# FFN gate and up products of a two-layer decoder: one 512-column pass of the high weights over both token parts, 128 inner columns at a time

## The chip, the cores and the metric

The kernel runs on one core of one Trainium2 chip. The metric is the device time of one execution in microseconds, median of several runs. Engines are named as in the profile: PE (TensorE matmul), PEld (TensorE weight load), DVE (VectorE), ACT (ScalarE), POOL (GpSimd), SP (the queue from which most DMAs are issued).

## What is computed

Two layers of a decoder trunk for 256 tokens of width 1024. Each layer has two feed-forward parts (FFN) with a token mixer between them; only the FFNs change here:

```python
def swiglu(x, w_gate, w_up, w_down):
    return (jax.nn.silu(x @ w_gate) * (x @ w_up)) @ w_down
# x: 256 x 1024; w_gate, w_up: 1024 x 2816; w_down: 2816 x 1024
f1 = swiglu(rms_norm(h, ffn1_pre_g[l]), ffn1_w_gate[l], ffn1_w_up[l], ffn1_w_down[l])
h = h + 0.5 * rms_norm(f1, ffn1_post_g[l])
```

Everything is float32, and the output must keep nearly its precision.

## The kernel before

**Split numbers.** A float32 product is made of three passes of TensorE. Each operand is split in a high part (rounded to the engine's reduced float32 format, `F32R`) and a low part (the rest), and high x high, high x low and low x high are summed in PSUM. `mm3` (L248) does that for products whose moving operand are weights; `gu_cols` (L372) does it where the weights are the stationary operand.

**Weights.** A unit is 1 MB of weights. SP fetches it into one of 3 raw buffers (`fetch`, L201); `prepare` (L215) splits it on ACT (copy to the high part, L227) and DVE (subtraction for the low part, L228), in pieces, into one of 5 ring slots. When TensorE has used a unit for the last time, `done` frees its slot and `pump` prepares and fetches the next, in the order of `specs`.

**Order.** TensorE's order is written by hand as strings (`FFN_FIRST`, `FFN_START`, `FFN_BODY`, `FFN_END`, and a loop at L413 to L417): each name is one step, run in that order. The orders of DVE and ACT are chosen by a scheduler at build time, the work on units at a lower priority; on the chip each engine runs its list strictly in order.

**The FFN.** The 2816 inner columns are 11 blocks of 256, numbered c = 0 to A (hexadecimal).

- c = 0 and 1 (`gu_rows`, steps g and u): the tokens are stationary (`xT`), the weights move; one step is one block of 256 columns for one of the two groups of 128 tokens. The outputs (`pg`, `pu`, one bank of 512 columns per token group) are evacuated by `evac_rows` and transposed by `tr`.
- c = 2 to A (`gu_cols`, steps G and U): the weights are stationary, 128 columns at a time (b = 0, 1), and all 256 tokens move. One step is 2 x 8 x 3 = 48 passes of 256 columns into one bank (`qg`, `qu`); `evac_cols` (step E) then works on 512 columns (both b) at a time and `split` leaves the two parts of `hT`.
- D steps (`down`): 12 passes of 512 columns for one block and one token group, into four banks `facc` that stay for the whole FFN. PSUM has 8 banks, so 4 are left for the rest.

Between FFNs stand the mixers, whose code the change does not touch.

At the start, `x0`, the first unit, `x1` (the second 128 tokens) and the second unit are fetched in this order (L953 to L960); the first unit by one DMA per 128 rows.

Of the kernel before, what the change touches and what calls it, by code (L numbers as in the profile page):

```python
# [14 lines left out]
AF = mybir.ActivationFunctionType  # L15
ALU = mybir.AluOpType
# [3 lines left out]
P = 128  # L20
D = 1024
KD = D // P
S = 256
# [18 lines left out]
"""  # L42
FFN_FIRST = "g00 xb1 g10 g01 g11 sc0 sc1 u00 u01 u10 u11 e0 e1"
FFN_START = "g00 g10 sc0 xb1 u00 u10 e0 g01 g11 sc1 u01 u11 e1"
FFN_BODY = "G2 t0 rsb U2 t1 E2 side D00 D01 D10 D11 G3 U3 E3 D20 D21"
FFN_END = "D80 D90 DA0 fa0 D81 D91 fb0 xb0 DA1 fa1 fb1"
NC = FF // 256

# [38 lines left out]
def trunk(ctx: ExitStack, tc: tile.TileContext, T, out):  # L87
# [54 lines left out]
    def ffn_specs(l, f):  # L142
        wg, wu, wd = (T[f"ffn{f}_w_{n}"][l] for n in ("gate", "up", "down"))

        def gu(nm, c):
            cols_unit((l, f, nm, c), wg if nm == "g" else wu, 0, KD, c * 256, 256)

        def dn(c):
            cols_unit((l, f, "d", c), wd, 2 * c, 2, 0, D)

        for nm in "gu":
            for c in range(2):
                gu(nm, c)
        for c in range(2, NC):
            gu("g", c)
            gu("u", c)
            if c == 2:
                dn(0)
                dn(1)
            elif c < NC - 1:  # L160
                dn(c - 1)
        dn(NC - 2)
        dn(NC - 1)
# [163 lines left out]
    def ffn(l, f, rs, finish, side=None):  # L327
        hr, ev = {}, {}

        def scales(t):  # L330
            hr[t], ev[t] = small("hr", 1), small("ev", 1)
            pool.tensor_scalar(hr[t], rs[t][0], 0.5, None, op0=ALU.mult)
            pool.tensor_scalar(ev[t], rs[t][1], 4.0 * EPS, None, op0=ALU.mult)

        acc = [None, None]
        ps, hT, hs, tmp = {}, {}, {}, {}


        def gu_rows(nm, c, t):
            if c == 0:  # L340
                ps[nm, t] = bank("p" + nm)
            u = units[l, f, nm, c]
            mm3(ps[nm, t][:, c * 256:(c + 1) * 256],
                [(xT[:, 0, t, k, :], xT[:, 1, t, k, :], u[:, 0, k, :], u[:, 1, k, :]) for k in range(KD)],
                True, True)
            if t == 1:
                done((l, f, nm, c))

        def evac_rows(t):
            g, u = ps.pop(("g", t)), ps.pop(("u", t))  # L350
            th = w(t, "th")
            act.activation(th, g, AF.Tanh, scale=hr[t])
            m = w(2 + t, "m")
            dve.scalar_tensor_tensor(m, th, 1.0, g, op0=ALU.add, op1=ALU.mult)
            h = w(4 + t, "h")
            dve.scalar_tensor_tensor(h, u, hr[t], m, op0=ALU.mult, op1=ALU.mult)
            hs[t] = h

        def split(src):
            q = half("hT").rearrange("p (h n) -> p h n", h=2)  # L360
            act.activation(q[:, 0], src, AF.Copy)
            dve.tensor_sub(q[:, 1], src, q[:, 0].bitcast(F32))
            return q

        def tr(t):
            b = bank("ht")
            for k in range(4):
                pe.transpose(b[:, k * P:(k + 1) * P], hs[t][:, k * P:(k + 1) * P], ident)
            hT[t] = split(b)


        def gu_cols(nm, c):  # L372
            o = bank("q" + nm)
            u = units[l, f, nm, c]
            for b in range(2):
                bs = slice(b * P, (b + 1) * P)
                o3 = o[:, b * 256:(b + 1) * 256].rearrange("p (t n) -> p t n", t=NT)
                n = 0
                for k in range(KD):
                    for a, h in ((0, 0), (0, 1), (1, 0)):  # L380
                        pe.matmul(o3, u[:, a, k, bs], xT[:, h, :, k, :], start=n == 0, stop=n == 3 * KD - 1)  # L381
                        n += 1
            ps[nm] = o
            done((l, f, nm, c))

        def evac_cols(c):
            i = c % 2
            b2 = lambda a: a.rearrange("p (b n) -> p b n", b=2)
            g, u = ps.pop("g"), ps.pop("u")
            gp = w(i, "gp")  # L390
            dve.tensor_tensor(b2(gp), b2(g), tmp["rsB"][:, None, :].to_broadcast([P, 2, S]), op=ALU.mult)  # L391
            m = w(2 + i, "m")
            act.activation(m, gp, AF.Tanh, scale=0.5)
            dve.scalar_tensor_tensor(m, m, 1.0, gp, op0=ALU.add, op1=ALU.mult)
            h = w(4 + i, "h")
            dve.scalar_tensor_tensor(h, u, 0.5, m, op0=ALU.mult, op1=ALU.mult)  # L396
            hT["c", c] = split(h)

        def down(c, t):
            if acc[t] is None:  # L400
                acc[t] = acc_tile("facc")
            u = units[l, f, "d", c]
            if c < 2:
                q = [[hT[t][:, a, (2 * c + k) * P:(2 * c + k + 1) * P] for k in range(2)] for a in range(2)]
            else:
                q = [[hT["c", c][:, a, k * 256 + t * P:k * 256 + (t + 1) * P] for k in range(2)] for a in range(2)]
            for j, js in enumerate(HALF):
                mm3(acc[t][j], [(q[0][k], q[1][k], u[:, 0, k, js], u[:, 1, k, js]) for k in range(2)],
                    c == 0, c == NC - 1)
            if t == 1:  # L410
                done((l, f, "d", c))

        order = (FFN_FIRST if side else FFN_START).split() + FFN_BODY.split()  # L413
        for c in range(4, NC):
            order += [f"{n}{c:X}" for n in "GUE"]
            if c < NC - 2:
                order += [f"D{c - 1:X}0", f"D{c - 1:X}1"]  # L417
        order += FFN_END.split()
        for n in order:
            if n == "rsb":  # L420
                tmp["rsB"] = broadcast_rows(rs)
            elif n == "side":
                if side:
                    side()
            elif n[:2] == "fa":
                finish[0](int(n[2]), acc[int(n[2])], ev[int(n[2])])
            elif n[:2] == "fb":
                finish[1](int(n[2]))
            elif n[:2] == "sc":
                scales(int(n[2]))  # L430
            elif n[:2] == "xb":
                if n[2] == "1" or not finish[2]:
                    pre_b(int(n[2]))
            elif n[0] in "gu":
                gu_rows(n[0], int(n[1]), int(n[2]))
            elif n[0] == "e":
                evac_rows(int(n[1]))
            elif n[0] == "t":
                tr(int(n[1]))
            elif n[0] in "GU":  # L440
                gu_cols(n[0].lower(), int(n[1], 16))
            elif n[0] == "E":
                evac_cols(int(n[1], 16))
            else:
                down(int(n[1], 16), int(n[2]))

# [572 lines left out]
```

## Time and profile before

| | |
|---|---|
| median of 3 runs | 994.09 us (992.03 to 998.48) |
| the profiled execution | 992.19 us, of which the profile's span 990.3 us |
| PE busy | 971.3 us (98%), 6678 matmuls |
| DVE busy | 646.6 us (65%) |
| ACT busy | 478.5 us (48%) |
| DMA | 176.04 MB, mean 178 GB/s |
| granted TensorE clock | 0.998 of full |

A matmul's duration in the profile overlaps with the next one's, so what a matmul costs is read from the distance between starts (the pitch), not from its duration. "Busy" of PE counts such overlapped time once.

### The profile page before, as it was taken

Reading aid. Unit: us, or ns where it says so; the run is one execution under the profiler, and the core shown is the slowest. Engines: PE = TensorE matmul, PEld = TensorE weight load, DVE = VectorE, ACT = ScalarE, POOL = GpSimd, SP = SyncE. Lnnn points to the kernel's source line nnn. Section 1 sums busy time; section 2 is a strip of 40 time slices with the busy share of each in tenths; the row PEclk is TensorE's granted clock in tenths of the full one; section 3 lists DMA queues with packets and bytes.
Section 4 is the critical chain, followed back from the end, with each engine's and each line's share of the span. In section 5 each row is a group of like instructions: output and inputs, shape, how many; then the busy total and the mean of one; then the engine's idle time right before and its main releaser. Section 6 shows DMA issues by size and latency. Waiting matters only on the chain.

```text
span 990.3 us, 16105 instructions
## 1 busy us (share of the span) xinstructions
PE 971.3 (98%) x6678; PEld 888.8 (90%) x6678; DVE 646.6 (65%) x864; ACT 478.5 (48%) x760; POOL 80.3 (8%) x136
## 2 busy tenths in 40 slices
PE   6999999999999999999999999999999999999997
PEld 6999999988779999999999999998887799999996
DVE  5785555578988655555677455567799776565552
ACT  5564343457556543443455343345468454443431
POOL 2000000030034000000030000002101320000000
PEclk9999999999999999999999999999999999999999
DMA  7975555456525555555557555553763166655511
GB/s 257 331 227 207 172 201 181 151 163 178 173 72 212 191 190 175 186 195 172 169 174 251 180 189 185 173 204 107 204 189 107 46 211 234 197 186 176 190 61 43
DMA packets 131553, 176.04 MB, mean 178 GB/s; under 512 B 13156, under 2 KB 111768, under 8 KB 131480
## 3 DMA queue, kind: packets, MB, share of 16 engines
q1 hardware_dynamic: 131192, 174.43, 53.6%
q8 instruction: 52, 0.85, 0.3%
q10 hardware_dynamic: 288, 0.59, 0.2%
q14 instruction: 21, 0.17, 0.0%
HBM read 173.95 MB, written 1.05 MB: 177 GB/s over the span
## 4 chain that ended last, share of the span: by engine, by line
PE 94%; DVE 2%; ACT 2%; DMA 1%; issue 0%; SPq 0%; DVEq 0%; POOLq 0%; POOL 0%; ACTq 0%
PE qu L381 21%; PE qg L381 21%; PE facc L251 8%; PE facc L252 8%; PE facc L253 8%; PE pu L251 2%; PE pu L253 2%; PE pu L252 2%; PE pg L252 2%; PE oacc L251 2%; PE pg L253 1%; PE oacc L253 1%; PE oacc L252 1%; PE pg L251 1%; PE yT L766 1%; PE chp L794 1%
## 5 line engine op out<-in xcount | busy, mean ns | idle before, releaser
L227 ACT ACTIVATE unit<-raw 128x1024 fp32r<-128x1024 f32 (+2 forms) x320 | 322.4, 1032 | 357.3 <-issue 301.1
L228 DVE TENSOR_TENSOR unit<-raw,unit 128x1024 fp32r<-128x1024 f32 (+2 forms) x320 | 375.9, 1195 | 138.6 <-ACT unit L227 138.2
L381 PEld LDWEIGHTS qg<-xT,unit 128*128 128x128 f32 x1728 | 211.6, 192 | 2.2
L381 PE MATMUL qu<-xT,unit 128*128 128x256 f32 x1728 | 213.5, 283 | 0.0
L381 PE MATMUL qg<-xT,unit 128*128 128x256 f32 x1728 | 213.0, 283 | 0.0
L381 PEld LDWEIGHTS qu<-xT,unit 128*128 128x128 f32 x1728 | 209.9, 192 | 0.0
L251 PE MATMUL facc<-unit,hT 128*128 128x512 f32 x352 | 137.9, 392 | 0.0
L252 PE MATMUL facc<-unit,hT 128*128 128x512 f32 x352 | 137.3, 390 | 0.0
L253 PE MATMUL facc<-unit,hT 128*128 128x512 f32 x352 | 137.0, 389 | 0.0
L253 PEld LDWEIGHTS facc<-unit,hT 128*128 128x128 f32 x352 | 66.1, 188 | 14.1
L251 PEld LDWEIGHTS facc<-unit,hT 128*128 128x128 f32 x352 | 66.2, 188 | 12.7
L252 PEld LDWEIGHTS facc<-unit,hT 128*128 128x128 f32 x352 | 66.2, 188 | 12.5
L391 DVE TENSOR_TENSOR gp<-qg,rsB 128x512 f32<-128x512 f32 x36 | 24.9, 690 | 67.5 <-PE qg L381 67.5
L396 DVE SCALAR_TENSOR_TENSOR h<-qu,m 128x512 f32<-128x512 f32 x36 | 24.9, 691 | 55.0 <-PE qu L381 55.0
L267 POOL TENSOR_TENSOR mspost<-ev,s 128x1 f32<-128x1 f32 x8 | 4.7, 589 | 677.1 <-ACT sq L261 677.1
L252 PE MATMUL pg<-unit,xT 128*128 128x256 f32 x128 | 37.4, 292 | 1.3 <-DVE unit L228 1.2
L251 PE MATMUL pg<-unit,xT 128*128 128x256 f32 x128 | 37.4, 292 | 0.3 <-ACT unit L227 0.3
L253 PE MATMUL pg<-unit,xT 128*128 128x256 f32 x128 | 37.0, 289 | 0.0
L251 PE MATMUL pu<-unit,xT 128*128 128x256 f32 x128 | 36.5, 285 | 0.0
L253 PE MATMUL pu<-unit,xT 128*128 128x256 f32 x128 | 36.2, 283 | 0.0
L252 PE MATMUL pu<-unit,xT 128*128 128x256 f32 x128 | 36.2, 283 | 0.0
L742 ACT ACTIVATE pr<-s,mx 128x128 f32<-128x128 f32 (+1 forms) x64 | 26.1, 433 | 3.0 <-DVE mx L740 2.9
(259 smaller groups left out, 1162.6 us busy)
## 6 DMA issues: line engine op xcount, KB each, us to landing
raw<-in_ffn_w_down_dram SPq DMA_DIRECT2D x44, 1024.0 KB, 5.1
raw<-in_ffn_w_gate_dram SPq DMA_DIRECT2D x42, 1024.0 KB, 5.0
raw<-in_ffn_w_up_dram SPq DMA_DIRECT2D x42, 1024.0 KB, 5.1
raw<-in_w_in_dram SPq DMA_DIRECT2D x14, 1024.0 KB, 5.1
raw<-in_w_out_dram SPq DMA_DIRECT2D x4, 1024.0 KB, 4.9
raw<-in_w_out_dram SPq DMA_DIRECT2D x8, 512.0 KB, 6.3
raw<-in_w_in_dram SPq DMA_DIRECT2D x4, 560.0 KB, 3.7
raw<-in_ffn_w_up_dram SPq DMA_DIRECT2D x4, 512.0 KB
```

What stands on the lines that cost most here:

```text
L227: act.activation(u[:, 0, i:i + step], r[:, i:i + step], AF.Copy)
L228: dve.tensor_sub(u[:, 1, i:i + step], r[:, i:i + step], u[:, 0, i:i + step].bitcast(F32))
L251: pe.matmul(o, sh, mh, start=first and i == 0, stop=False)
L252: pe.matmul(o, sh, ml, start=False, stop=False)
L253: pe.matmul(o, sl, mh, start=False, stop=last and i == n - 1)
L267: pool.tensor_add(m, eps, s2[:, 0:1])
L381: pe.matmul(o3, u[:, a, k, bs], xT[:, h, :, k, :], start=n == 0, stop=n == 3 * KD - 1)
L391: dve.tensor_tensor(b2(gp), b2(g), tmp["rsB"][:, None, :].to_broadcast([P, 2, S]), op=ALU.mult)
L396: dve.scalar_tensor_tensor(h, u, 0.5, m, op0=ALU.mult, op1=ALU.mult)
L742: act.activation(prs[v][:, b0 + i, :], sb[v][:, i, :], AF.Exp, bias=mx[:, i:i + 1], accum_out=cf[:, v, b0 + i:b0 + i + 1])
L766: pe.matmul(YT[t][v * 64:(v + 1) * 64, :], vsw[kb][:, br, v * 64:(v + 1) * 64], PT.pop((t, br, v, kb)), start=False, stop=br == 1 and kb == t,
L794: pe.matmul(b3, u[:, a, k, cs_], xT[:, h, :, k, :], start=n == 0, stop=n == 3 * KD - 1)
```

## The change

For c = 2 to A, each b now is a step of its own (G20, U20, E20, G21, ...). For each of the 8 row blocks k, the low weights meet the high tokens in a pass of 256 columns, and the high weights meet the high and the low tokens in one pass of 512 columns; the two products lie side by side in one bank and are added when it is evacuated: ACT copies the second half out, DVE adds the first. `evac_cols` works on 256 columns at a time. A unit of gate or up weights is used by two steps and freed after the second.

For c = 0 and 1, the two units of gate (and of up) are the upper and the lower half of the rows, 512 columns wide, in place of two blocks of 256 columns over all rows; `gu_rows` makes passes of 512 columns.

```diff
-FFN_BODY = "G2 t0 rsb U2 t1 E2 side D00 D01 D10 D11 G3 U3 E3 D20 D21"
+FFN_BODY = "G20 t0 rsb U20 E20 G21 t1 U21 E21 side D00 D01 D10 D11 G30 U30 E30 G31 U31 E31 D20 D21"
@@ ffn_specs
-            for c in range(2):
-                gu(nm, c)
+            for h in range(2):
+                cols_unit((l, f, nm, h), wg if nm == "g" else wu, 4 * h, 4, 0, 512)
@@ gu_rows
-            u = units[l, f, nm, c]
-            mm3(ps[nm, t][:, c * 256:(c + 1) * 256],
-                [(xT[:, 0, t, k, :], xT[:, 1, t, k, :], u[:, 0, k, :], u[:, 1, k, :]) for k in range(KD)],
-                True, True)
+            u = units[l, f, nm, h]
+            mm3(ps[nm, t], [(xT[:, 0, t, 4 * h + k, :], xT[:, 1, t, 4 * h + k, :], u[:, 0, k, :], u[:, 1, k, :])
+                            for k in range(4)], h == 0, h == 1)
@@ gu_cols
-            for b in range(2):
-                bs = slice(b * P, (b + 1) * P)
-                o3 = o[:, b * 256:(b + 1) * 256].rearrange("p (t n) -> p t n", t=NT)
-                n = 0
-                for k in range(KD):
-                    for a, h in ((0, 0), (0, 1), (1, 0)):
-                        pe.matmul(o3, u[:, a, k, bs], xT[:, h, :, k, :], start=n == 0, stop=n == 3 * KD - 1)
-                        n += 1
+            bs = slice(b * P, (b + 1) * P)
+            for k in range(KD):
+                pe.matmul(o[:, :S].rearrange("p (t n) -> p t n", t=NT), u[:, 1, k, bs], xT[:, 0, :, k, :],
+                          start=k == 0, stop=False, skip_group_check=True)
+                pe.matmul(o.rearrange("p (h t n) -> p h t n", h=2, t=NT), u[:, 0, k, bs], xT[:, :, :, k, :],
+                          start=False, stop=k == KD - 1, skip_group_check=True)
@@ evac_cols
-            dve.tensor_tensor(b2(gp), b2(g), tmp["rsB"][:, None, :].to_broadcast([P, 2, S]), op=ALU.mult)
-            m = w(2 + i, "m")
+            act.activation(gp, g[:, S:], AF.Copy)
+            act.activation(h, u[:, S:], AF.Copy)
+            dve.tensor_add(gp, g[:, :S], gp)
+            dve.tensor_mul(gp, gp, tmp["rsB"])
             act.activation(m, gp, AF.Tanh, scale=0.5)
+            dve.tensor_add(h, u[:, :S], h)
             dve.scalar_tensor_tensor(m, m, 1.0, gp, op0=ALU.add, op1=ALU.mult)
-            dve.scalar_tensor_tensor(h, u, 0.5, m, op0=ALU.mult, op1=ALU.mult)
-            hT["c", c] = split(h)
+            dve.scalar_tensor_tensor(h, h, 0.5, m, op0=ALU.mult, op1=ALU.mult)
+            split(h, hT["c", c][:, :, bs])
@@ the loop over c = 4 to A
-            order += [f"{n}{c:X}" for n in "GUE"]
+            order += [f"{n}{c:X}{b}" for b in range(2) for n in "GUE"]
```

On PE, at a block in the middle of an FFN, one row of before stands for 48 equal passes (`unit_860` is the block's gate unit, `unit_901` its up unit, `unit_957` a down unit):

```order
L252 MATMUL facc_704<-unit_804,hT_874 128x512
L253 MATMUL facc_704<-unit_804,hT_874 128x512
L381 MATMUL qg_1061<-xT_80,unit_860 128x256 x48
L381 MATMUL qu_1117<-xT_80,unit_901 128x256 x48
L251 MATMUL facc_689<-unit_957,hT_1027 128x512
```

After the change, the same place where step G of b = 0 ends and U of b = 0 begins (`unit_601` is the gate unit, `unit_632` the up unit):

```order
L378 MATMUL qg_776<-xT_80,unit_601 128x256
L380 MATMUL qg_776<-xT_80,unit_601 128x512
L378 MATMUL qu_793<-xT_80,unit_632 128x256
L380 MATMUL qu_793<-xT_80,unit_632 128x512
L378 MATMUL qu_793<-xT_80,unit_632 128x256
```

Each step now alternates 8 passes of 256 and 8 of 512 columns, and a block has four steps (G, U, G, U) in place of two.

On ACT, one block of before (the pieces of three units, L227, stand around the two steps of the evacuation):

```order
L227 ACTIVATE unit_1569<-raw_1421 128x1024
L227 ACTIVATE unit_1625<-raw_1477 128x1024
L361 ACTIVATE hT_1639<-h_1637 128x512
L227 ACTIVATE unit_1625<-raw_1477 128x1024
L227 ACTIVATE unit_1666<-raw_1518 128x1024 x2
```

and a block of the change, from the end of b = 0 to the end of b = 1:

```order
L361 ACTIVATE hT_950<-h_949 128x256
L393 ACTIVATE gp_947<-qg_961 128x256
L227 ACTIVATE unit_978<-raw_846 128x1024 x2
L397 ACTIVATE m_948<-gp_947 128x256
L394 ACTIVATE h_949<-qu_985 128x256
L227 ACTIVATE unit_1002<-raw_870 128x1024 x2
L361 ACTIVATE hT_950<-h_949 128x256
L227 ACTIVATE unit_1043<-raw_911 128x1024 x2
```

The copies out of the banks (L393, L394) are new, and the last part of b = 1 (L361) stands behind both pieces of a unit. From the first `facc` evacuation of an FFN to the first step of the next FFN, the lists of DVE and ACT are the same as before.

On SP, at the start of the program, before:

```order
L953 DMA x0_81<-in_x_dram 128x1024
L210 DMA raw_99<-in_ffn1_w_gate_dram 128x256 x5
L210 DMA raw_99<-in_ffn1_w_gate_dram 128x256 [waits DMAHW0_49]
L210 DMA raw_99<-in_ffn1_w_gate_dram 128x256 [waits DMAHW1_49]
L210 DMA raw_99<-in_ffn1_w_gate_dram 128x256 [waits DMAHW2_49]
L957 DMA x1_82<-in_x_dram 128x1024 [waits DMAHW3_49]
L210 DMA raw_109<-in_ffn1_w_gate_dram 128x4x256 [waits DMAHW4_49]
```

and after (a name behind "waits" is one of eight counters, freed by the landing of an earlier DMA):

```order
L957 DMA x0_81<-in_x_dram 128x1024
L210 DMA raw_99<-in_ffn1_w_gate_dram 128x512 x4
L961 DMA x1_82<-in_x_dram 128x1024
L210 DMA raw_105<-in_ffn1_w_gate_dram 128x2x512 [waits DMAHW0_49]
L210 DMA raw_105<-in_ffn1_w_gate_dram 128x2x512 [waits DMAHW1_49]
```

The first unit is now four DMAs, and `x1` is issued without a wait.

## Rows read from the trace of the kernel before

**Rows 1.** The page's part 1: busy time, share of the span, instructions, by engine.

```profile
PE 971.3 (98%) x6678; PEld 888.8 (90%) x6678; DVE 646.6 (65%) x864; ACT 478.5 (48%) x760; POOL 80.3 (8%) x136
```

**Rows 2.** The page's part 4: the chain that ended last, by engine.

```profile
PE 94%; DVE 2%; ACT 2%; DMA 1%; issue 0%; SPq 0%; DVEq 0%; POOLq 0%; POOL 0%; ACTq 0%
```

**Rows 3.** Waits of PE, whole span: line, releaser, us in total, times, longest us.

```profile
PE xt L311 <- DMA cn<-in_consts_dram: 6.8, 1, 6.8
PE yT L720 <- ACT pcT L715: 2.4, 2, 1.2
PE pg L252 <- DVE unit L228: 1.2, 2, 1.0
```

**Rows 4.** Chain in order of time, one block c: start us, length us, what.

```profile
78.34 5.75 PE qg L381 x48
84.09 5.76 PE qu L381 x48
95.32 5.75 PE qg L381 x48
```

**Rows 5.** Timeline of PE: first and twelfth of a row of 512-column passes.

```profile
300.05 0.39 PE L251 MATMUL oacc<-unit,yA 128*128 128x512 f32 x1
...
302.55 0.39 PE L253 MATMUL oacc<-unit,yL 128*128 128x512 f32 x1
```

**Rows 6.** Windows, one block c: stretch, length, busy by engine, clock, DMA share, GB/s.

```profile
78.30:95.30 17.00, 17.00 (x123) 16.04 (x122) 9.67 (x10) 7.07 (x8) 0.00 (x0) 1.00 0.54 187
```

**Rows 7.** Timeline of PE: first and 34th of a row of gu_rows passes.

```profile
19.03 0.28 PE L253 MATMUL pg<-unit,xT 128*128 128x256 f32 x1
...
22.99 0.28 PE L253 MATMUL pg<-unit,xT 128*128 128x256 f32 x1
```

**Rows 8.** Groups by line and shape: count, busy us, mean ns, idle before, releaser.

```profile
L228 DVE TENSOR_TENSOR unit<-raw,unit 128x1024 fp32r<-128x1024 f32 x304 | 365.0, 1221 | 133.2 <-ACT unit L227 132.9
L391 DVE TENSOR_TENSOR gp<-qg,rsB 128x512 f32<-128x512 f32 x36 | 24.9, 690 | 67.5 <-PE qg L381 67.5
L394 DVE SCALAR_TENSOR_TENSOR m<-m,gp 128x512 f32<-128x512 f32 x36 | 24.7, 685 | 4.2 <-ACT m L393 4.2
L842 DVE SCALAR_TENSOR_TENSOR xc<-xr,prm,xc 128x256 f32<-128x256 f32 x12 | 5.7, 477 | 0.1
L570 DVE TENSOR_TENSOR qr<-qA,qB 128x256 f32<-128x256 f32 x4 | 1.7, 419 | 0.0
L798 DVE TENSOR_TENSOR gl<-chg,rsB 128x256 f32<-128x256 f32 x4 | 1.7, 414 | 0.3 <-PE chg L794 0.3
L393 ACT ACTIVATE m<-gp 128x512 f32<-128x512 f32 x36 | 22.2, 618 | 10.8 <-DVE gp L391 10.7
L361 ACT ACTIVATE hT<-h 128x512 fp32r<-128x512 f32 x36 | 22.1, 614 | 5.1 <-DVE h L396 5.1
L323 ACT ACTIVATE rsB<-rsB 128x256 f32<-128x256 f32 x6 | 2.3, 380 | 0.0
L856 ACT ACTIVATE thi<-gate,hb 128x256 f32<-128x256 f32 x4 | 1.9, 475 | 1.1 <-DVE e L854 1.1
```

**Rows 9.** Timeline, end of the first FFN: first pass of D80, last part of hT.

```profile
186.11 0.40 PE L251 MATMUL facc<-unit,hT 128*128 128x512 f32 x1
...
188.59 0.69 DVE L362 TENSOR_TENSOR hT<-h,hT 128x512 fp32r<-128x512 f32 x1
```

**Rows 10.** Timeline of ACT: a unit's piece right behind the end of step G.

```profile
118.14 1.06 ACT L227 ACTIVATE unit<-raw 128x1024 fp32r<-128x1024 f32 x1 [3.75 <-issue]
```

**Rows 11.** Chain in order of time, the start of the program.

```profile
7.30 5.81 DMA x<-in_x_dram
13.32 0.48 issue
13.80 0.69 DVE xg L278
14.49 0.61 DVE unit L228
15.15 0.38 PE pg L252
```

**Rows 12.** Timeline of SP, and of PE at the first up pass.

```profile
1.16 6.09 SPq L210 DMA_DIRECT2D raw<-in_ffn_w_gate_dram  x8
7.30 0.44 SPq L957 DMA_DIRECT2D x<-in_x_dram  x1
...
25.63 0.28 PE L251 MATMUL pu<-unit,xT 128*128 128x256 f32 x1
```

**Rows 13.** Windows, the start: stretch, length, busy by engine, clock, DMA share, GB/s.

```profile
11.00:13.00 2.00, 2.00 (x11) 2.00 (x11) 0.69 (x2) 0.73 (x3) 1.04 (x4) 1.00 1.07 365
```

More of the change, by code (lines that the diff above doesn't have):

```diff
@@ L336, in ffn, with gu_rows @@
         ps, hT, hs, tmp = {}, {}, {}, {}
-        def gu_rows(nm, c, t):
-            if c == 0:
+        def gu_rows(nm, h, t):
+            if h == 0:
                 ps[nm, t] = bank("p" + nm)
-            u = units[l, f, nm, c]
-            mm3(ps[nm, t][:, c * 256:(c + 1) * 256],
-                [(xT[:, 0, t, k, :], xT[:, 1, t, k, :], u[:, 0, k, :], u[:, 1, k, :]) for k in range(KD)],
-                True, True)
+            u = units[l, f, nm, h]
+            mm3(ps[nm, t], [(xT[:, 0, t, 4 * h + k, :], xT[:, 1, t, 4 * h + k, :], u[:, 0, k, :], u[:, 1, k, :])
+                            for k in range(4)], h == 0, h == 1)
             if t == 1:
-                done((l, f, nm, c))
+                done((l, f, nm, h))
         def evac_rows(t):
@@ L357, in evac_rows, with split @@
             hs[t] = h
-        def split(src):
-            q = half("hT").rearrange("p (h n) -> p h n", h=2)
+        def split(src, q=None):
+            if q is None:
+                q = half("hT").rearrange("p (h n) -> p h n", h=2)
             act.activation(q[:, 0], src, AF.Copy)
@@ L369, in tr, with gu_cols @@
             hT[t] = split(b)
-        def gu_cols(nm, c):
-            o = bank("q" + nm)
+        def gu_cols(nm, c, b):
+            o = ps[nm] = bank("q" + nm)
             u = units[l, f, nm, c]
-            for b in range(2):
-                bs = slice(b * P, (b + 1) * P)
-                o3 = o[:, b * 256:(b + 1) * 256].rearrange("p (t n) -> p t n", t=NT)
-                n = 0
-                for k in range(KD):
-                    for a, h in ((0, 0), (0, 1), (1, 0)):
-                        pe.matmul(o3, u[:, a, k, bs], xT[:, h, :, k, :], start=n == 0, stop=n == 3 * KD - 1)
-                        n += 1
-            ps[nm] = o
-            done((l, f, nm, c))
@@ L389, in evac_cols @@
+            if b == 1:
+                done((l, f, nm, c))
+        def evac_cols(c, b):
+            if b == 0:
+                i = c % 2
+                tmp["w"] = w(i, "gp"), w(2 + i, "m"), w(4 + i, "h")
+                hT["c", c] = half("hT").rearrange("p (h n) -> p h n", h=2)
+            bs = slice(b * S, (b + 1) * S)
+            gp, m, h = (a[:, bs] for a in tmp["w"])
             g, u = ps.pop("g"), ps.pop("u")
-            gp = w(i, "gp")
-            dve.tensor_tensor(b2(gp), b2(g), tmp["rsB"][:, None, :].to_broadcast([P, 2, S]), op=ALU.mult)
@@ L440, in ffn @@
             elif n[0] in "GU":
-                gu_cols(n[0].lower(), int(n[1], 16))
+                gu_cols(n[0].lower(), int(n[1], 16), int(n[2]))
             elif n[0] == "E":
-                evac_cols(int(n[1], 16))
+                evac_cols(int(n[1], 16), int(n[2]))
             else:
```

4 lines of the change are left out of this document (removed).

## The prediction

> **What bounds the kernel now.** I first read the busy shares: PE is busy for 98% of the span, DVE for 65%, ACT for 48% [rows 1]. The chain of work that ended last is PE for 94% [rows 2], and PE's waits sum to little: 6.8 us for the first data, and some 6 us more in the whole span, none inside an FFN after the start [rows 3]. So time falls only where PE's own stream gets shorter, as long as the others keep up. The next question is what a pass costs. Its duration in the profile overlaps with the next one's, so I take the pitch. One step G of 48 passes of 256 columns lasts 5.75 us [rows 4], which is 119.9 ns a pass. Twelve passes of 512 columns start between 300.05 and 302.55 [rows 5]: 2.50 / 11 = 227.3 ns. The D steps of a block agree: from 84.09 + 5.76 = 89.85 to 95.32 are 5.47 us for 24 passes [rows 4], 227.9 ns with the turn to the next step.
>
> At 2.4 GHz (the granted clock of this block is 1.00 [rows 6]) 256 columns stream in 106.7 ns and 512 in 213.3. So a pass costs its columns plus 13 to 14 ns, whether it is short or long. Two passes of 256 cost 239.8 ns, one of 512 costs 227.3: each such pair that becomes one pass saves 12.5 ns. The number of columns that stream does not change; only the number of passes does.
>
> **The term of the change, on PE.**
> - c = 2 to A: 4 FFNs x 9 blocks x 2 (gate, up) x 2 (b) x 8 (k) = 1152 times, three passes of 256 become one of 256 and one of 512: 1152 x 12.5 ns = 14.4 us. A block loses 0.40 us of its 16.98 [rows 4].
> - c = 0 and 1: 4 FFNs x 2 x 2 token groups x 2 units x 24 = 768 passes of 256 become 384 of 512: 384 x 12.5 ns = 4.8 us. Their pitch now is the same as in the blocks: 33 steps between 19.03 and 22.99 are 120.0 ns each [rows 7].
> - Sum 19.2 us. With 227.9 ns for a 512 pass it is 1536 x 11.9 = 18.3; inside a D step alone the pitch would allow 19.5.
>
> What is not in the trace is a 512 pass whose moving rows are four separate pieces of 128 (high and low part, two token groups). Today's block passes read two pieces (119.9 ns), those of `gu_rows` one (120.0), with no difference between them; so I price four pieces at nothing extra. The other unseen thing is the alternation of short and long passes. The turns from G/U to D and back (two per block) are inside the 5.47 us and cost at most 24 x 0.6 ns = 14 ns together, so I take nothing there either.
>
> The Trainium skill speaks against this change. "TensorE: Matmul & The Clock Gate", section "Wait — 56ns, not 53.3ns?", gives the warm pitch as N / 2.4 GHz plus about 2.5 ns. By it 256 columns cost 109.2 ns and 512 cost 215.8, a pair saves 2.5 ns and the whole change 3.8 us, too little to be seen. The trace does not agree: 119.9 and 227.3 ns. I follow the rows; a pass with hardly a cost of its own is the first rival.
>
> **What is added on DVE and ACT, and what hides it.** Per block DVE had four operations of 512 columns at about 688 ns [rows 8], 2.75 us. Now it has six of 256 per b; by the nearest rows 3 x 0.414 (sums and the scaling, L798, L570), 2 x 0.477 (L842) and 0.419 for the low part: 2.62 us, 5.24 per block, 2.5 more, 90 us over 36 blocks. ACT had 0.618 + 0.614; now per b two copies at 0.380 (L323), a tanh at 0.475 (L856) and a copy at 0.380: 3.23 per block, 2.0 more, 72 us in all. A block today has 9.67 us of DVE and 7.07 of ACT in 17.0 [rows 6]; it becomes 12.2 and 9.1 in 16.6. The tightest place is c = 9 and A, which have no D steps between: 11.1 us with two units (9.67 - 2.75 = 6.92 us for three, 2.31 each) and 5.24 of evacuation, 9.9 us, 89%. So both stay under PE and I price them at nothing; beyond that, each microsecond by which a block is late would be one on the path.
>
> Waits: four PSUM banks rotate among G, U, G, U, so a step needs the bank of the step four before it, which ended 8.3 us earlier or more. The evacuation of a bank stands behind at most one unit (two pieces: 1.06 each on ACT [rows 10], 1.22 on DVE [rows 8]), so it takes 3 to 5 us. At the end of an FFN the last hT part is needed by the fourth pass of DA0, 5.46 + 0.68 us after the last U. Today it is ready at 188.59 + 0.69, 3.2 us behind 186.11 [rows 9]; then it stands behind both pieces of a unit on ACT, and by the same rows I get 4.5 to 4.7 us. No wait, 1.5 us to spare.
>
> Ring slots: the gate unit is freed after G of b = 1, 8.3 us into the block instead of 5.76, the up unit at 11.1 as before. Today ACT starts the next unit right when G ends (118.14 [rows 10]), so its data had landed. The slot freed by gate takes the down unit that is needed 16 us after its new preparation; nothing there comes onto the path.
>
> **The start.** x1 is issued at 7.30, behind eight pieces of the first unit of which the later ones wait for counters, and lands 5.81 us later [rows 11, 12]. DVE's work on x1 (`xg`) then stands before the last piece of the first unit, which PE awaits at 15.15. After: five issues at about 0.44 us [rows 12] put x1 at about 3 us. Ahead of it are the gains, x0 and the first unit, 2.1 MB with a little, and itself 0.5 MB; at the 365 GB/s of this stretch [rows 13] that is some 7 us, so I expect it at about 10. On the other side DVE now has two pieces, not one, behind `xg`. Worked through (xg from 11.0, third piece at 12.9, g00 done at 15.1), the first up pass comes at about 24.2 instead of 25.63 [rows 12]; 0.45 of this is already in the 4.8. I take 1 us. If x1 comes no sooner, PE waits for the third piece until 15.1 and the start loses 1 us; if nothing waits, it gains 2.5.
>
> **Sum.** 990.3 - 19.2 - 1.0 = 970.1 us of span; with the 1.9 us around it 972.0. The profiled execution lies 1.9 us under the median of the runs shown, so a median should lie between 972 and 974: I say 973.
>
> **Rivals.**
> 1. *The saving per pass is not there.* The excess is not a pass's own but follows something that stays (the split products summed, the rows read), and the new pair takes what the three passes took, 359.7 ns. For it: no row shows the same stream both ways. Against: 256 and 512 columns show the same excess, 13.2 and 14.0 ns, so an excess that grows with columns is excluded. Time: only the start is left, 992.2 - 1 = 991, by the median 993: no change that can be seen. The Trainium skill's 2.5 ns a pass ("TensorE: Matmul & The Clock Gate") would make it 987 to 989, no change either.
> 2. *The long pass hides more.* If the excess came from loading weights behind a short pass, a pass of 512 would have none, and a triple would cost its 768 columns, 320 ns instead of 359.7: 1152 x 39.7 = 46 us, time 940 to 947. Against: today's 512 passes still carry 14 ns.
> 3. *Evacuation comes late.* ACT and DVE run in order; a unit whose data is late holds the copy out of a bank behind it. With 0.53 us of wait per block the 19 us are gone; half of that gives 982. For it: 89% of DVE at c = 9 and A. Against: the 8.3 us above.
> 4. *Slower: four pieces cost.* If reading high and low tokens from far-apart rows cost a restart per piece, the 512 pass in qg and qu would be dearer. From 227.3 + 16.7 = 244 ns on, the gain is gone (1152 x 16.7 ns = 19.2 us); at 252 it is slower by 1%, about 1002. Against: one piece and two cost the same [rows 4, 7].
>
> **How the numbers follow.** A measurement of this kernel tells about 1% from no change (10 us). Chances: the forecast 0.80 (968 to 978: 18.3 to 19.5 for the passes, -1 to +2.5 for the start, 972 to 974 for the median, and some scatter), rival 1 0.07, rival 2 0.03, rival 3 0.06, rival 4 0.04. Faster by over 1% is the forecast, rival 2 and most of rival 3: 0.87; same is rival 1 and the rest of 3: 0.09; slower 0.04. The range 965 to 982 holds the forecast, with room for its scatter, and the milder half of rival 3.
>
> **What the changed profile would show.** Right: a block c lasts about 16.6 us instead of 16.98, a step G of 16 passes about 2.78 us, matmuls 6678 - 1536 = 5142, DVE near 735 us, ACT near 550, no new waits of PE inside the FFNs, up passes starting at about 24. Wrong would be: blocks at 16.9 (rival 1), at 15.7 (rival 2), PE waiting for `qg` or `qu` banks or for `hT` (rival 3), or 512 passes in qg at over 240 ns (rival 4).

## The result, and the profile after

The changed kernel takes 983.03 us (median, 982.67 to 983.91) against 993.94 us of the kernel before (992.03 to 998.48) on the same chip: a ratio of 0.989, 95% interval 0.987 to 0.9911. It is faster by 10.9 us; the prediction said 973 us, 21 us faster, and 965 to 982 as the range. About half of the expected gain is there. One of the ten runs of an experiment below (the long pass as two short ones) took 1753.75 us at a mean granted clock of 0.78; no ratio here counts it.

The profiled execution took 983.91 us, of which the span is 982.0 us (before 990.3). The page of the kernel after, part 1, and PE's waits (line, releaser, us in total, times, longest us):

```profile
PE 963.9 (98%) x5142; PEld 807.9 (82%) x5142; DVE 716.5 (73%) x1152; ACT 543.0 (55%) x976; POOL 81.2 (8%) x136
```

```profile
PE xt L311 <- DMA cn<-in_consts_dram: 7.5, 1, 7.5
PE yT L724 <- ACT pcT L719: 2.1, 2, 1.2
PE cmpT L678 <- DVE kcb L670: 1.0, 2, 0.6
PE pT L759 <- DVE pr L751: 0.8, 2, 0.4
PE pg L251 <- ACT unit L227: 0.4, 1, 0.4
```

There are 5142 matmuls, as counted in advance, and PE is still busy for 98% of the span [rows 1]. Every wait has its like before, and none lies inside an FFN after the start [rows 3]. So the missing gain is inside PE's own stream. The timeline of PE in a step G of the kernel after (start us, duration us, what) shows it:

```profile
110.14 0.28 PE L378 MATMUL qg<-xT,unit 128*128 128x256 f32 x1
110.26 0.40 PE L380 MATMUL qg<-xT,unit 128*128 128x512 f32 x1
110.49 0.28 PE L378 MATMUL qg<-xT,unit 128*128 128x256 f32 x1
110.61 0.40 PE L380 MATMUL qg<-xT,unit 128*128 128x512 f32 x1
110.85 0.28 PE L378 MATMUL qg<-xT,unit 128*128 128x256 f32 x1
...
111.20 0.28 PE L378 MATMUL qg<-xT,unit 128*128 128x256 f32 x1
...
112.97 0.28 PE L378 MATMUL qu<-xT,unit 128*128 128x256 f32 x1
```

Read the distances between starts. A pair of a short and a long pass takes 0.35, 0.36, 0.35 us and so on; eight pairs from 110.14 to 112.97 are 2.83 us, 353.8 ns a pair. The prediction had 119.9 + 227.3 = 347.2, and the three passes of before took 359.7. So a pair saves 6 ns, not 12.5. The whole block shows the same (window of one block's length, with length, busy time of PE, PEld, DVE, ACT and POOL, granted clock, DMA share, GB/s):

```profile
110.77:127.56 16.79, 16.79 (x90) 14.30 (x89) 11.64 (x18) 8.90 (x15) 0.00 (x0) 1.00 0.57 188
```

It lasts 16.79 us, where 16.98 stood before [rows 4] and 16.58 was expected. DVE has 11.64 us of work in it and ACT 8.90: both have room.

**Where the time went.** The second FFN from its first pass on `pg` to its last on `facc`, after and then before:

```profile
308.43 0.39 PE L251 MATMUL pg<-unit,xT 128*128 128x512 f32 x1
...
494.67 0.39 PE L253 MATMUL facc<-unit,hT 128*128 128x512 f32 x1
```

```profile
309.79 0.28 PE L251 MATMUL pg<-unit,xT 128*128 128x256 f32 x1
...
499.11 0.39 PE L253 MATMUL facc<-unit,hT 128*128 128x512 f32 x1
```

186.24 us and 189.32: 3.08 us less, where 4.8 were expected. With the same two marks the trace splits the whole span (us):

| | before | after | difference | expected |
|---|---|---|---|---|
| to the first `pg` pass | 9.13 | 9.82 | +0.69 | } -5.8 |
| FFN 1 | 193.99 | 190.31 | -3.68 | } |
| FFN 2, 3, 4 | 567.09 | 557.83 | -9.26 | -14.4 |
| mixer 1 | 106.67 | 108.29 | +1.62 | 0 |
| mixer 2 | 106.46 | 109.03 | +2.57 | 0 |
| the rest | | | -0.2 | 0 |
| span | 990.3 | 982.0 | -8.3 | -20.2 |

Three things are short: each FFN by 1.7 us (6.9 together), the start by about 1 us, and both mixers, whose code did not change, are longer by 4.2 us together. In the mixers the granted clock fell; the experiment on the clock, below, shows that this lengthened them. The window of the kernel after around the place where it lost most (same columns), and the chain of waits there:

```profile
745.00:756.00 11.00, 11.00 (x51) 6.04 (x51) 7.74 (x17) 5.51 (x17) 0.00 (x0) 0.69 0.28 95
```

```profile
732.48 1.06 PE s L740 x8
...
744.73 1.12 PE yT L724 x2
...
750.88 2.01 PE s L740 x8
```

The eight passes of L740 take 1.06 us at 732 and 2.01 us at 751, with a mean granted clock of 0.69 between 745 and 756: part of it at 2.4, part at 1.2 GHz. Just ahead PE had waited 1.18 us for ACT (L724). The same place in the profiled run of before has the same wait ahead of `yT` (timeline, first line), but the eight passes behind it (chain, second) last 1.06 us, and the granted clock (window, third) is 1.00:

```profile
752.28 1.12 PE L720 MATMUL yT<-pcT,vb 32*128 32x512 f32 x2 [1.18 <-ACT pcT L715]
```

```profile
756.51 1.06 PE s L736 x8
```

```profile
725.00:760.00 35.00, 32.95 (x248) 27.08 (x247) 33.09 (x66) 24.18 (x66) 0.00 (x0) 1.00 0.50 151
```

### The profile page after: what moved, and what is told of

The parts are those of the page before. It is cut to its first block, busy times and chain, and to the rows that moved or that the text cites. A ratio compares the mean times of both kernels' runs of the same rounds, so it can differ in the third digit from the quotient of the medians.

```text
span 982.0 us, 13520 instructions
## 1 busy us (share of the span) xinstructions
PE 963.9 (98%) x5142; PEld 807.9 (82%) x5142; DVE 716.5 (73%) x1152; ACT 543.0 (55%) x976; POOL 81.2 (8%) x136
## 4 chain that ended last, share of the span: by engine, by line
PE 93%; DVE 3%; ACT 2%; DMA 1%; issue 0%; DVEq 0%; POOLq 0%; ACTq 0%; POOL 0%
PE qg L380 14%; PE qu L380 14%; PE facc L252 8%; PE facc L251 8%; PE facc L253 8%; PE qg L378 7%; PE qu L378 7%; PE oacc L251 2%; PE pg L252 2%; PE oacc L253 1%; PE pu L251 1%; PE oacc L252 1%; PE pu L253 1%; PE pu L252 1%; PE pg L253 1%; PE pg L251 1%
## 5 line engine op out<-in xcount | busy, mean ns | idle before, releaser
L227 ACT ACTIVATE unit<-raw 128x1024 fp32r<-128x1024 f32 (+2 forms) x320 | 315.3, 1032 | 105.5 <-PE facc L253 62.9
L380 PE MATMUL qg<-xT,unit 128*128 128x512 f32 x576 | 206.8, 398 | 0.0
L380 PE MATMUL qu<-xT,unit 128*128 128x512 f32 x576 | 206.2, 398 | 0.0
L378 PE MATMUL qu<-xT,unit 128*128 128x256 f32 x576 | 162.3, 282 | 0.0
L378 PE MATMUL qg<-xT,unit 128*128 128x256 f32 x576 | 161.7, 281 | 0.0
L380 PEld LDWEIGHTS qu<-xT,unit 128*128 128x128 f32 x576 | 108.2, 188 | 26.4
L378 PEld LDWEIGHTS qu<-xT,unit 128*128 128x128 f32 x576 | 108.8, 189 | 0.0
L252 PEld LDWEIGHTS facc<-unit,hT 128*128 128x128 f32 x352 | 66.1, 188 | 14.4
L361 ACT ACTIVATE hT<-h 128x256 fp32r<-128x256 f32 x72 | 30.1, 419 | 60.9 <-DVE h L400 60.9
L393 ACT ACTIVATE gp<-qg 128x256 f32<-128x256 f32 x72 | 27.7, 384 | 62.9 <-PE qg L380 62.5
L395 DVE TENSOR_TENSOR gp<-qg,gp 128x256 f32<-128x256 f32 x72 | 30.3, 421 | 33.5 <-ACT gp L393 33.5
L397 ACT ACTIVATE m<-gp 128x256 f32<-128x256 f32 x72 | 29.7, 412 | 40.5 <-DVE gp L396 40.4
L398 DVE TENSOR_TENSOR h<-qu,h 128x256 f32<-128x256 f32 x72 | 30.3, 421 | 27.1 <-ACT h L394 27.1
```

The costliest lines, as they stand in the source:

```text
L227: act.activation(u[:, 0, i:i + step], r[:, i:i + step], AF.Copy)
L252: pe.matmul(o, sh, ml, start=False, stop=False)
L378: pe.matmul(o[:, :S].rearrange("p (t n) -> p t n", t=NT), u[:, 1, k, bs], xT[:, 0, :, k, :], start=k == 0, stop=False, skip_group_check=True)
L380: pe.matmul(o.rearrange("p (h t n) -> p h t n", h=2, t=NT), u[:, 0, k, bs], xT[:, :, :, k, :], start=False, stop=k == KD - 1, skip_group_c ...
L393: act.activation(gp, g[:, S:], AF.Copy)
L395: dve.tensor_add(gp, g[:, :S], gp)
```

## The experiments

The theories on the 6 ns by which a pair is dearer than the prediction had it. **A**: a change between a short and a long pass costs time on PE by itself. **B**: the new work on ACT and DVE beside it (reads of the banks) slows the passes. **D**: what runs ahead of a step decides. And on the mixers, **C**: they are longer because of the clock alone. Theory F was formed on the way, below. Medians are set against runs of the kernel before on the same chip; a time without an interval is that of one execution. "FFN 2" below is the stretch defined above, which repeats to 0.1 us between kernels whose passes are the same.

### Long and short passes apart

```diff
             for k in range(KD):
                 pe.matmul(o[:, :S]..., u[:, 1, k, bs], xT[:, 0, :, k, :], ...)
+            for k in range(KD):
                 pe.matmul(o..., u[:, 0, k, bs], xT[:, :, :, k, :], ...)
```

> The changed kernel, but each step G and U makes its 8 passes of 256 columns first and then its 8 passes of 512, instead of taking turns. Theory A (turns): the pair costs 353 ns instead of the 347 I had summed because short and long passes take turns. Then a step falls from 2.825 us to 8 x 120 + 8 x 227 = 2.78 us, and the kernel by 144 x 0.048 = 7 us, to 976. Theory B (company): the passes are slower because ACT and DVE now read more PSUM while PE writes it. Then the sum of a step stays at 2.82 us and the kernel at 983.

Measured: 974.39 us (973.66 to 976.53), ratio 0.9805 [0.9774, 0.9835]; 174.6 ns a pass, and FFN 2 lasts 184.85 us. ACT and DVE have the same work, so B falls here. Timeline of PE, one step with its passes merged (the last six of the eight short ones, then the eight long ones):

```profile
109.89 0.88 PE L378 MATMUL qg<-xT,unit 128*128 128x256 f32 x6
110.61 2.00 PE L381 MATMUL qg<-xT,unit 128*128 128x512 f32 x8
112.45 1.12 PE L378 MATMUL qu<-xT,unit 128*128 128x256 f32 x8
```

The short ones start 120 ns apart (six in 110.61 - 109.89 = 0.72 us). The long ones take 1.84 us, 230 ns each: the first start 234 and 235 ns apart, the last 226 and 227. So after a turn from short to long the first two passes are some 7 to 9 ns dear, and the pitch settles after five.

### One part of the change at a time

Rows alone: the kernel before with the `ffn_specs` and `gu_rows` parts of the diff, `gu_cols` and `evac_cols` as before.

> The kernel before with only the first 512 inner columns changed (halves of the rows, passes of 512). Both theories: 384 passes fewer at 227 ns for two of 120, 4.9 us, and nothing at the start: 989. If the start does help as I predicted: 988.

Columns alone: the changed kernel with c = 0 and 1 as before.

> The changed kernel with the first 512 inner columns as before. Theory A and B: 1152 pairs that save 6.5 ns each, 7.5 us: 986.5. If the mixers lose time through a lower granted clock that depends on when they begin (theory C), the clock record of the profile shows it, and the time is up to 4 us more.

Measured: 988.92 us (986.26 to 990.48), ratio 0.9946 [0.9927, 0.9964], and 986.15 us (984.84 to 986.65), ratio 0.9917 [0.9887, 0.9947]. FFN 2 lasts 188.11 and 187.45 us: the rows take off 1.22 us an FFN (1.2 expected), the columns 1.88 (3.6 expected). The two add up to 3.10, the 3.08 of the change to within the reading. So the rows' term holds, and the whole shortfall of the FFNs sits in the alternating pairs.

### The long pass as two short ones

```diff
-                pe.matmul(o..., u[:, 0, k, bs], xT[:, :, :, k, :], ...)
+                for h in range(2):
+                    pe.matmul(o[:, h * S:(h + 1) * S]..., u[:, 0, k, bs], xT[:, h, :, k, :], ...)
```

> The changed kernel, but the 512-column pass of a pair is made as two passes of 256, one for each half of the bank; steps, evacuation and use of units are those of the change. Theory A: a pass costs 120 ns as before, so a step lasts 24 x 0.120 = 2.88 us and the kernel takes what the rows-only kernel takes, 989. Theory B: the passes stand in the same company of ACT and DVE and are slower than before, 122 ns or more, and the kernel takes 994 or more.

Measured: 989.11 us, ratio 0.995 [0.9932, 0.9968]; FFN 2 is 188.11 us, the same as with rows alone. A triple starts every 0.36 us:

```profile
109.86 0.28 PE L378 MATMUL qg<-xT,unit 128*128 128x256 f32 x1
109.97 0.40 PE L381 MATMUL qg<-xT,unit 128*128 128x256 f32 x2
110.21 0.28 PE L378 MATMUL qg<-xT,unit 128*128 128x256 f32 x1
...
110.57 0.28 PE L378 MATMUL qg<-xT,unit 128*128 128x256 f32 x1
```

The banks, the evacuation and the alternation of low and high weights are those of the change, and the passes cost what they cost before. So the new steps, the freeing of units and the work of ACT and DVE (rival 3 and theory B) cost nothing that shows; the dear thing is a length of 512 beside one of 256.

### The long pass first

```diff
+                pe.matmul(o..., u[:, 0, k, bs], xT[:, :, :, k, :], ...)
                 pe.matmul(o[:, :S]..., u[:, 1, k, bs], xT[:, 0, :, k, :], ...)
-                pe.matmul(o..., u[:, 0, k, bs], xT[:, :, :, k, :], ...)
```

> The changed kernel with the two passes of each pair in the other order, 512 columns first. Theory A (turns): a step has as many turns between short and long passes as before, so a pair stays at 353 ns and a step at 2.82 us. If only the order within a pair mattered, a pair would come to 347 ns and a step to 2.77 us.

Measured: 978.75 us, both mixers at full clock (106.71 and 106.49 us long). The steps are at 176.4 ns a pass and FFN 2 at 186.25 us, as in the changed kernel. The order inside a pair is no matter. Its mixers are 4.1 us shorter than those of the changed kernel's profiled run, and that is most of the difference.

### Four transposes ahead of each step

```diff
+            for k in range(4):
+                pe.transpose(o[:, k * P:(k + 1) * P], ident, ident)
             for k in range(KD):
```

> The changed kernel with four extra transposes of 128 columns on PE ahead of every step G and U (their output is overwritten by the step). They cost 144 x 4 x 0.109 = 63 us. In the changed kernel the two steps that follow transposes ran at 173.6 ns a pass, all others at 176.5. Theory D: what ran ahead of a step decides how its turns go; then all steps run at 173.5 and the time is 983 + 63 - 7 = 1039. Theory A alone (each turn costs its 6.4 ns whatever ran ahead): steps stay at 176.5, 1046.

Measured: 1036.65 us; this is extra work, and the steps are what counts. A step of 20 takes 161.2 x 20 = 3224 ns, and behind the transposes the pairs run like this:

```profile
116.77 0.28 PE L380 MATMUL qg<-xT,unit 128*128 128x256 f32 x1
116.88 0.39 PE L382 MATMUL qg<-xT,unit 128*128 128x512 f32 x1
117.11 0.28 PE L380 MATMUL qg<-xT,unit 128*128 128x256 f32 x1
...
118.50 0.28 PE L380 MATMUL qg<-xT,unit 128*128 128x256 f32 x1
```

Five pairs from 116.77 to 118.50 are 346 ns each. This is strict alternation, with as many turns as in the changed kernel, at the price that the prediction gave it. So A in its simple form, a fixed price for a turn, falls, and D holds in part. In the changed kernel itself the steps at c = 2 behind the transposes of `t0` (U20, then G21) show the same 347.

### Two by two, and the fewest turns

Two by two: 256, 256, 512, 512. Fewest turns: in G the eight long passes first, in U the eight short ones, so that G ends and U begins with short ones.

> The changed kernel with two passes of 256, then two of 512, and so on: half the turns. Theory A: the extra of a step falls with the turns, but a long run of 512 after a turn showed its extra over about five passes (234, 235, 229, 232, 231 ns, then 227), so two of 512 keep most of it: 4 x 2 x 8 = 64 down to 30 ns a step, 175 to 176.5 ns a pass, against 174.6 with eight and eight. A cost per turn alone, 6.4 ns: 175.0.

> As the grouped kernel, but step G makes its long passes first and U its short ones first, so that a block has two ways from short to long instead of four. Theory A: each way costs 20 ns (27 over the eight long passes, 7 back on the first short one), so a block falls by 0.04 us and the kernel by 1.4 us, 973 against 974.4 of the grouped one; the steps average 173.4 ns a pass.

Measured: two by two 975.18 us at 174.2 ns a pass, FFN 2 184.63; fewest turns 974.94 (973.21 to 975.76), ratio 0.9814 [0.9786, 0.9842], at 174.0 on average, FFN 2 184.47. Two by two turns from short to long four times in a step, where the grouped kernel does so once, and its FFN is no longer; so it is not the number of turns that counts. Its 174.2 ns lie below both values foreseen. Fewest turns has FFNs 0.38 us shorter than the grouped kernel, 1.5 us in four where 1.4 were expected; its median does not show that. The 173.4 ns expected of its steps don't fit that sum: 40 ns less over a block's 64 passes is 0.6 off 174.6, which is the 174.0 measured.

### The rhythm of a row of pairs

To the tenth of a microsecond all this looks like one price; start by start there are two patterns. Behind the transposes the distances are 230, 117, 230, 117 ns (346.7 a pair). In the changed kernel they are 232, 118, 240, 120, 236, 114 and then again from the start: three pairs in 1060 ns, 353.3 each. So the theory became **F**: a row of alternating passes keeps the pattern in which it was entered. The next three put extra transposes ahead of G of b = 0 alone (four, as in the diff, then one), and one ahead of every step.

```diff
+            for k in range(4 if nm == "g" and b == 0 else 0):
+                pe.transpose(o[:, k * P:(k + 1) * P], ident, ident)
             for k in range(KD):
```

> Four extra transposes ahead of step G of b = 0 alone (36 times), the passes as in the changed kernel. The trace of the kernel with four transposes ahead of every step shows the alternating passes in a steady rhythm of 117 and 230 ns (346.7 a pair), the changed kernel shows another of three pairs (232 and 118, 240 and 120, 236 and 114: 353.3 a pair). Theory F (the engine keeps the rhythm with which it enters a row of alternating passes): all four steps of the block run at 173.4 ns a pass; an FFN after the first lasts 186.24 - 288 x 0.0063 + 9 x 0.44 = 188.4 us. Theory D' (only what stands right ahead of a step counts): the first step of four runs at 173.4, the others at 176.5, and the FFN lasts 189.8. If the transposes do nothing here: 176.5 in all, 190.2.

> One extra transpose (about 109 ns) ahead of step G of b = 0. Theory F with any short pass as the trigger: all steps of a block at 173.4 ns a pass, an FFN after the first 186.24 - 1.8 + 1.0 = 185.4 us. If one transpose does not set the steady rhythm: 176.5 and 187.2 us.

> One extra transpose ahead of each step. With one as a sufficient trigger: 173.4 ns a pass and an FFN of 186.24 - 1.8 + 36 x 0.109 = 188.4 us; if it is not one: 176.5 and 190.2 us.

Measured: FFN 2 lasts 189.15, 186.13 and 189.83 us (whole times 992.35, 983.19 and 994.76 with the extra work). The first two lie midway between the outcomes foreseen, the third near that of one transpose not being enough. With four or one ahead of a block, the blocks take turns. With one, here is step U of b = 0 in one block, then the same step in the next block:

```profile
114.05 0.28 PE L380 MATMUL qu<-xT,unit 128*128 128x256 f32 x1
114.17 0.40 PE L382 MATMUL qu<-xT,unit 128*128 128x512 f32 x1
114.41 0.28 PE L380 MATMUL qu<-xT,unit 128*128 128x256 f32 x1
...
115.83 0.28 PE L380 MATMUL qg<-xT,unit 128*128 128x256 f32 x1
```

```profile
129.83 0.28 PE L380 MATMUL qu<-xT,unit 128*128 128x256 f32 x1
129.94 0.39 PE L382 MATMUL qu<-xT,unit 128*128 128x512 f32 x1
130.17 0.28 PE L380 MATMUL qu<-xT,unit 128*128 128x256 f32 x1
...
132.60 0.28 PE L380 MATMUL qg<-xT,unit 128*128 128x256 f32 x1
```

From 114.05 to 115.83 are five pairs in 1.78 us, 356 ns each at this resolution; over whole steps the first block has 177.2, 176.5 and 176.3 ns a pass. From 129.83 to 132.60 are eight pairs in 2.77 us, 346 ns each, and the three steps have 173.4, 173.3 and 173.3. Later blocks go on in this alternation up to c = 8. The instructions are the same, the granted clock too, and the pattern is kept through all of a block's steps. So one part of F is shown: strict alternation has two patterns, 6.7 ns a pair apart, and mostly stays in the one that it is in. Its other part, that the transposes set the pattern, failed: the same instructions stand ahead of a slow block and of a fast one, so they alone don't pick it. The kernel with one transpose ahead of each step shows both patterns as well, and changes of pattern inside a step. Transposes are no good as a remedy, as one costs about 0.1 us and doesn't choose reliably.

What picks a pattern, and what makes it inside the engine, isn't settled. The distances of even rows, 120.0 and 226.7 ns, and the sums 346.7 and 353.3 are 18, 34, 52 and 53 times 6.67 ns, so the slow pattern is one such piece longer in each pair; that is an observation, not a cause.

### The clock in the mixers

```diff
             YT[t] = bank("yT")
+            for _ in range(5):
+                pe.matmul(YT[t], xT[:, 0, 0, 0, :], xT[:, 0, 0, 0:4, :]..., start=True, stop=True, ...)
```

> The changed kernel with five extra passes of 512 columns (about 1.14 us of work whose result is overwritten) on TensorE ahead of step co0/co1 of the mixers, where it waits 1.18 us for ACT (L719). Theory C (the 4.3 us that the two mixers cost more in the profiled run of the changed kernel come from the clock that falls there, 0.69 granted between 745 and 756): with the wait filled the clock stays at 1.00 in that stretch, 990-type low clocks go, mixers return to 109 us each, and the median falls from 983.0 to 980-981. If the clock falls for another reason (the sparse passes of 32 columns behind it, or by chance from run to run), the median stays at 983 +- 1 and the low stretch stays. The steps in the FFNs stay at 176.5 ns a pass by every theory.

Measured: 982.24 us (981.48 to 982.3), ratio 0.9882 [0.9859, 0.9905]. The same window as above, now with the wait filled:

```profile
745.00:756.00 11.00, 11.00 (x84) 8.35 (x81) 10.57 (x22) 8.31 (x21) 1.40 (x1) 1.00 0.31 97
```

The granted clock stays at 1.00 there, as C says. In all five runs its mean over the program was 0.998 or 0.999; in the four of the changed kernel it was 0.993 to 0.995, in eleven of the kernel before on this chip 0.992 to 0.999, with 991.5 us at 0.999 and 997.5 at 0.992. The time that C foresaw, 980 to 981, did not come; the median lies in the band of the rival (983 +- 1). The filling itself costs: two of its four places have no wait, and the mixers last 107.36 and 108.50 us at full clock, 0.7 and 2.0 more than those of before.

What bears C out is how long a mixer lasts in every trace. In the fourteen traces without the filling there are three values: 106.4 to 106.7 us (both of before; both of the grouped kernel and of long-first), 108.1 to 108.4 (both of rows alone), and 109.0 to 109.4 (mixer 2 of the changed kernel, mixer 1 of columns alone). The clock record of the traces has no fall in any mixer of the first kind, a short one in each of the second and a longer one in each of the third. The same instructions fall into one or another from run to run: the two-by-two kernel had 106.70 and 108.17 in one run, 108.38 and 108.12 in another. So the mixers' extra time is the clock's; why it falls in one run and not in another isn't shown.

### Two by two again, and with the wait filled

> The two-by-two kernel (256, 256, 512, 512 in each step) timed. By its single look (975.2) and its steps of 174.2 ns a pass: 1152 pairs x (353.0 - 348.4) = 5.3 us and the D steps' 1.1 to 1.3 ns for 864 passes, 1.0 us, under the changed kernel: 983.0 - 6.3 = 976.7; less some 2 us if the clock in the mixers does not fall: 974.5. Range 974 to 977.5, against 974.4 of the grouped kernel. A fixed price for each turn between short and long would have it at 979 to 980 (half the turns of the changed kernel, half of the way to the grouped one).

> Two by two, and the five extra passes in the mixers' wait. Theory C: 972.5 to 974.5, 1 to 2 us under the two-by-two kernel without them, and less scatter. If the filling does nothing to the clock: the same as that kernel within 0.7 us, or up to 0.3 us longer.

Measured: 975.26 us (974.69 to 976.49), ratio 0.9816 [0.979, 0.9842], and 975.45 (974.83 to 975.9), ratio 0.9815 [0.979, 0.9841]. The filled one is not faster, against the 1 to 2 us expected: in its trace no mixer has a fall, and they last 107.35 and 108.52 us, against 108.38 and 108.12 with a fall in each without the filling. The five passes cost what they save. Grouped, two by two and fewest turns cannot be told apart by their medians (974.39, 975.26, 974.94); each beats the change by about 8 us and the kernel before by about 19.

## Why the prediction was right or wrong

**Right: what bounds it, and what a pass costs.** Each pass costs its columns plus some 13 ns, and fewer passes make it faster. Rows alone gave 1.22 us an FFN for 1.2, the 512 passes of a grouped step go down to 227 ns, and FFN 2 of the fewest-turns kernel is 4.86 us shorter for the 4.8 of the sum. The four separate pieces that a long pass reads cost nothing. Rival 1 (the saving is not there) falls with that. The Trainium skill ("TensorE: Matmul & The Clock Gate", section "Wait — 56ns, not 53.3ns?") gives about 2.5 ns as a pass's own cost; by it the estimate for the grouped kernel is a gain of 4 us, and it gained 19, so the measurement decides against that figure here. Rival 2 (a pair for the price of its columns) falls with 347 ns as the lowest.

**Wrong: the alternation.** The step that failed is this sentence: "The turns from G/U to D and back (two per block) are inside the 5.47 us and cost at most 24 x 0.6 ns = 14 ns together, so I take nothing there either." What was measured there was two turns a block; the change makes two in every pair, and that step was not taken. The price was read too low as well: start by start, the first five passes of a 24-pass D run of before are 234, 235, 229, 232 and 231 ns apart and the rest 226.7, some 28 ns dear in all, of which the first short passes behind give back some 8. A row of 32 alternating pairs is a stream that no row of before showed, and it can run in a pattern of 353.3 ns. In the changed kernel it does in 32 of the 36 blocks throughout, and in part of the other four (c = 2). The term was 1152 x 12.5 = 14.4 us; measured are 4 x 1.88 = 7.5. As it was named as unseen, its bounds should have been worked out: nothing on the one side, and on the other the 14 ns of a block's two turns for each pair, 1152 x 14 ns = 16 us, which leads to 989 us. That range would have held the result.

**Wrong: the clock in what doesn't change.** The sum took the mixers as fixed. In the profiled run they cost 4.2 us more, because the granted clock fell in them and had not in the profiled run of before. The prediction raised its sum by 1.9 us to get from that run to the median and left open where the scatter of before, 992.0 to 998.5, comes from. In the runs of before with a clock on record the time goes with it (991.5 us at 0.999, 997.5 at 0.992), though no trace of a long one is kept. The same chance strikes either kernel, and the mean clock of the changed one, 0.993 to 0.995, is low in all four runs. With its FFNs and full clock it would be about 983.9 - 4.2 = 979.7 us (the long-first kernel, which has both, took 978.75), inside the range; that would have been luck, with half of the columns' term still missing.

**The start: right about the queue, too high in the sum.** x1 is issued at 3.39 us instead of 7.30 [rows 12]; SP's rows of the kernel after:

```profile
1.17 2.18 SPq L210 DMA_DIRECT2D raw<-in_ffn_w_gate_dram  x4
3.39 0.47 SPq L961 DMA_DIRECT2D x<-in_x_dram  x1
```

Its work on DVE (`xg`) then starts at 12.29 instead of 13.80 [rows 11] and the third piece is there at 13.6 instead of 15.1. But the first up pass came at 25.18, only 0.45 before that of the kernel before, all of which the shorter passes explain. The chain of waits at that place, first of the kernel after and then of the fewest-turns kernel, where the up passes start at 24.0, tells why:

```profile
13.63 0.80 PE pg L252
14.43 0.43 PE pg L253
...
15.71 0.43 PE pg L253
16.14 0.99 PE xt L311 x8
17.13 0.23 PE pg L251
```

```profile
13.65 0.50 PE pg L252
14.15 0.23 PE pg L253
...
14.85 0.23 PE pg L253
15.09 0.87 PE xt L311 x8
15.96 0.23 PE pg L251
```

In the first, passes of 512 columns go on at 0.43 us, which is 512 columns at 1.2 GHz, until about 16 us; in the second they are at 0.23 from 14.15 on. The window of the first shows a granted clock of 1.00 all the same:

```profile
13.50:17.00 3.50, 3.42 (x15) 2.80 (x15) 3.18 (x6) 2.49 (x7) 3.26 (x6) 1.00 0.77 236
```

The clock record of a trace begins with this rise, at 16.25 us in the first and 13.58 in the second, and the window counts no loss ahead of it; here the passes' own pace is what tells. The prediction's 24.2 us came where the clock rose early: in the fourteen traces with the new start the up passes start at 23.8 to 24.2 us when it has risen by 14.2, and at 25.1 to 25.4 when it rises at 16.0 or later. Set beside an old start with the same rise, the new one is worth less than the sum had it: 24.00 against 24.63 of columns alone (rise at 13.58 and 13.55), 24.52 of two by two filled against 25.63 of before (14.61 and 14.48). That is 0.6 to 1.1 us, 0.45 of it the shorter passes', where the sum had 1.0 on top of them. The first pass on `pg` comes later with the new start in every trace, at 9.69 to 10.06 us instead of 9.13 and 9.38; why isn't shown. So the step was right about the queue and took the clock for granted. The Trainium skill ("TensorE: Matmul & The Clock Gate", section "What you observe") says that the moment at which the clock rises varies from run to run, by half a microsecond either way; these two vary by more, 2.7 us with the first passes on `pg` 0.02 us apart.

**Right: what hides the new work.** DVE 716.5 us (735 foretold), ACT 543.0 (550). No wait for a bank or for `hT` came up. At the end of the first FFN the last part of `hT` was ready at 187.43 + 0.42, 4.7 us behind the first pass of D80 at 183.13, as worked out (4.5 to 4.7). Rival 3 gave 982 us, nearly the time measured, but that is chance: the kernel with three short passes has all of its mechanism and loses nothing. Rival 4 put a dearer 512 pass on its pieces, and its mark, 240 ns and more, is touched by one long pass in three; the grouped kernel has the same pieces at 227 ns, so the pieces aren't it.

## What to carry to other kernels

Fewer, longer passes pay a fixed cost less often, but look at the order in which lengths follow each other: grouped or two by two kept nearly all of the gain here, and one by one lost half of what the columns should have given. A stream that no row of the old trace shows gets a bound on both sides, even if its parts are all known. Compare stretches of the same instructions (a whole FFN between two marks) rather than medians: they repeat to 0.1 us, while the clock moves the whole by several.

## What was not expected of the hardware

- A strict alternation of 256 and 512 columns runs in one of two patterns, 346.7 or 353.3 ns a pair, and mostly keeps it over dozens of pairs; what picks one isn't known, as either can follow the same instructions.
- Behind a turn from short to long the 512 passes are 234 and 235 ns apart and settle at 227 after five; a D run of 24 passes averages 227.8 ns in the kernel before, 228.7 in the changed one and 226.7 in the grouped one, where long passes stand ahead of it.
- The granted clock falls in the mixers in some runs and not in others, with the same instructions, for 1.6 to 2.7 us a mixer. With PE's 1.18 us wait filled it fell in neither of the two traces, and the mean over the program was 0.998 or 0.999 in all ten runs of the two kernels.
- In the first 13 to 17 us passes run at the 1.2 GHz pace (0.43 us for 512 columns) although the window's clock column shows 1.00 there, as in [rows 13]: the record begins only with the rise. The distances between passes are the better witness.
